# Glu product and the first depth half of MLP units two to four: one 512-column matmul with the weights' high part in place of two of 256

## The chip, the cores and the metric

The kernel runs on one core of one Trainium2 chip. The metric is the device time of one execution in microseconds, the median of several runs. TensorE (PE in the profile) multiplies, VectorE (DVE) and ScalarE (ACT) do the elementwise work, GpSimd (POOL) little, and SyncE (SP) issues most DMAs. PEld is PE's loading of weights, which overlaps its matmuls.

## The reference, cut to what matters

One decoder block on 256 tokens of width 2048, in float32: a state-space branch and an attention branch, gated and merged, then an MLP of width 8192, both behind RMS norms whose scale and shift come from a conditioning vector c.

```
mod = silu(c) @ w_ada + b_ada                 # sh1, sc1, g1, sh2, sc2, g2
h = rms_norm(x) * (1 + sc1) + sh1
u, q, k, v, ga, gb = split(h @ w_in)
y = gelu(ssm(u));  y_ssm = y * sigmoid(y @ w_glu + b_glu)      # w_glu: 1024 x 1024
merged = sigmoid(ga) * (y_ssm @ w_proj_ssm) + sigmoid(gb) * (attention(q, k, v) @ w_proj_attn)
x = x + g1 * (merged @ w_out)
h2 = rms_norm(x) * (1 + sc2) + sh2
x = x + g2 * (square(relu(h2 @ w_ff1)) @ w_ff2)                # w_ff1: 2048 x 8192
out = rms_norm(x)
```

## The kernel before, in words

**Products in two parts.** Every large product is taken in float32 parts that PE multiplies fast: a number is a high part (the rounded cast) plus a low part (what is left). Of the four part products three are summed: high x high, high weight x low activation, low weight x high activation. `split` (L179) makes the parts of a tile of weights: a cast on ACT (L184, whi) and a subtraction on DVE (L186, wlo).

**Weights as a stream.** `stream` (L190) loads a tile of 128 x 1024 float32 (512 KB, seven buffers wraw), splits it (four buffers each of whi and wlo) and yields it. Load and split get a priority of 300 (OFF) ahead of their place in the program. With a list of two depth tiles `load` (L170) takes 128 x 512 of each instead: the same 512 KB, in rows of 2 KB and not 4 KB. A tile scheduler of the language orders each engine's instructions by priority and by a model of their times; `after` pins one instruction behind another.

**Three forms of product.** They differ in which operand is held in the array and how wide the other one is.
- `steps_n` (L303) holds the activations and streams the weights, 512 columns.
- `steps_t` (L255, called by `gemm_t`) holds a 128 x 128 block of weights and streams the 256 tokens. A tile is eight blocks, three matmuls of 256 columns each: L270 whi x high activation, L271 whi x low activation, L272 wlo x high activation. Two blocks share a PSUM bank, so 1024 columns of weights take four banks.
- `gemm_d` (L279) holds a block of weights too, but streams high and low activations beside each other: L289 is one matmul of 512 columns with whi, L293 one of 256 with wlo, which lands on the second half of the bank. A bank then belongs to one block of 128 weight columns, so four banks hold 512 columns of weights, and the result is the sum of the bank's two halves. It takes the weights in pairs of depth tiles. Activations must lie as [depth tile, high/low, token].

**Banks.** `four` (L109) gives four banks. While `turn` is None they come from one rotation of five ("mm"); three others ("ax") are for transposes and the like. From L1683 on, groups alternate between four of the first kind and one of the first with the three others.

**Order of the program around the change.** After the input products and the attention and scan (to about 430 us): `proj_attn(0)` (L1402); the glu product (L1412, `gemm_t`, 8 tiles), whose banks go straight into sigmoids (L1418), a multiply (L1421) and a split into gg; `proj_attn(1)`; the product of gg with w_proj_ssm; w_out; then the MLP. Its first product is cut into eight units of 1024 columns. For the first four units (NP = 4) the first half of the depth is taken early, while the second half of the activations h2h is not there yet (loop at L1653): unit one (g = 0) over 4 depth tiles, before the shift is known, units two to four (g = 1 to 3) over 8 tiles with `gemm_t`. An ACT copy of 128 x 512 per bank (L1663) takes the result into `part`. The rest of the depth and the other units run later in `ff1` (L1545, `gemm_d`): there a unit is two groups of 512 columns, and its banks go out by an ACT copy of one half (L1557) and a DVE add of the other (L1558), or, onto a `part`, by two DVE adds (L1554, L1555).

**The conditioning beside it.** mod is worked out on DVE beside the products: a job of the lane "ada" loads 512 KB of w_ada and, one tile later, multiplies and sums it (L391). `step` (L155) runs after each tile of a stream and adds the lane's rate to its credit; a job starts per whole credit. The rates are constants: R4 for the 8 tiles of the last v product, RS0 for the 16 tiles of the next one, RS3 and RPA around glu, RM for units two to four. 96 jobs must be done before `make_h` (L1679) makes the second half of h2h; `flush` (L1677) issues what is left.

Of the kernel before, what the change touches and what calls it, by code (L numbers as in the profile page):

```python
# [13 lines left out]
F32R = mybir.dt.float32r  # L14
I32 = mybir.dt.int32
AF = mybir.ActivationFunctionType
# [3 lines left out]
P = 128  # L20
S = 256
# [26 lines left out]
R1 = .75  # L48
R2 = .75
R3 = .25  # L50
R4 = .7
R5 = .9
RS0 = .4
RSM = .2
RS2 = .25
RS3 = .7
# [2 lines left out]
RSS = .41  # L59
RPA = .6  # L60
RWO = .76
RM = 1.0
NP = 4
TW = 3
TF = 6
# [12 lines left out]
class Kern:  # L78
# [200 lines left out]
    def gemm_d(self, src, kts, c0, x2):  # L279
        nc = self.nc  # L280
        banks = self.four("pd")
        pairs = self.pairs(list(kts))
        n = len(pairs)
        for i, (ks, hi, lo) in enumerate(self.stream(src, pairs, c0)):
            last = i == n - 1
            cut = lambda blk, k: slice(512 * k + blk * P, 512 * k + (blk + 1) * P)

            def high(blk, k):
                nc.tensor.matmul(banks[blk], hi[:, cut(blk, k)], x2[:, ks[k], :, :], start=i + k == 0, stop=False,  # L289
                                 skip_group_check=True)  # L290

            def low(blk, k):
                self.mm = nc.tensor.matmul(banks[blk][:, S:2 * S], lo[:, cut(blk, k)], x2[:, ks[k], 0, :], start=False,  # L293
                                           stop=last and k == 1, skip_group_check=True)

            for blks in [(b,) for b in range(4)] if last else [range(4)]:
                for f in (high, low):
                    for blk in blks:
                        for k in range(2):
                            f(blk, k)  # L300
        return banks

    def steps_n(self, src, kts, c0, xh, xl, koff=0, tail=1, mid={}, homes=(), seed=None):  # L303
        nc = self.nc
# [705 lines left out]
    def body(self):  # L1010
        nc, a, v = self.nc, self.a, self.nc.vector
# [61 lines left out]
        with self.tc.high_priority(offset=OF1):  # L1073
# [15 lines left out]
            a2 = self.slot("A2", [P, KT, 2, S], F32R, name="ah")  # L1089
# [13 lines left out]
            h = self.big.tile([P, 2, S], F32, name="htmp", tag="htmp", bufs=1)[:, 0]  # L1103
# [140 lines left out]
        def qkvu(u, after=None, spare=False, mid={}):  # L1244
            which, g0, g1 = u
            self.spare = spare
            f = self.gemm_n if which in (2, 4) else self.gemm_t
            banks = f(*place(*u), self.ah, self.al, seed=seeds(which) if g0 else None, mid=mid)
            if after:
                self.prime(*place(*after))  # L1250
            evac(which, banks, g0)
# [88 lines left out]
        qkvu((1, 3, 3), (2, 3, 3))  # L1340
        self.lanes["ada"][1] = R4
        self.lane("tz", [lambda h=h: self.bias_load(h) for h in range(0, H, 2)], .4, .6)
# [28 lines left out]
        self.lane("m", heads[4:-4] + [table0] + heads[-4:] + [start] + bgl, RAT, 1.0)  # L1371
        self.lanes["ada"][1] = RS0

        for i in range(1, 4):
# [3 lines left out]
            banks = self.gemm_n(win, range(KT), c0, self.ah, self.al, tail=2)  # L1378
# [16 lines left out]
        def proj_attn(cg):  # L1395
            banks = self.gemm_n(a["w_proj_attn"][0], range(8), cg * 1024, yh, yl)
            for b in range(4):
                c = cg * 1024 + (b % 2) * 512
                d = gb[:, b // 2, c:c + 512]
                v.tensor_mul(d, d, banks[b])  # L1400

        proj_attn(0)  # L1402
        self.lanes["ada"][1] = RPA
        yy = self.slot("VT", [P, 2, 8, S], F32R, name="yy")
        yT = self.yT.rearrange("p s k c -> p k s c")
        sc4 = lambda z: z.rearrange("p k (c s) -> p k s c", s=4)
        self.gate, self.hgate = self.done[-4]
        for k in range(4):
            self.split(sc4(yy[:, 0, 2 * k:2 * k + 2]), sc4(yy[:, 1, 2 * k:2 * k + 2]), yT[:, 2 * k:2 * k + 2])
        self.gate = self.hgate = None  # L1410
        self.gates = [(None, None), self.done[-1]]
        banks = self.gemm_t(a["w_glu"][0], range(8), 0, yy[:, 0], yy[:, 1])  # L1412
        gg = self.slot("QT", [P, 2, 8, S], F32R, name="gg")
        sg = self.slot("S5", [P, 4, 2, S], name="sg")
        for b in range(4):
            t = sg[:, b]
            for k in range(2):
                nc.scalar.activation(t[:, k], banks[b][:, k * S:(k + 1) * S], AF.Sigmoid,  # L1418
                                     bias=self.bglu[:, 2 * b + k:2 * b + k + 1])
            s = slice(2 * b, 2 * b + 2)  # L1420
            v.tensor_mul(sc4(t), sc4(t), yT[:, s])  # L1421
            self.split(gg[:, 0, s], gg[:, 1, s], t)
        proj_attn(1)
        m2 = self.slot("A2", [P, 2, KT, S], F32R, name="mh")
        mh, ml = m2[:, 0], m2[:, 1]
# [11 lines left out]
        for cg in range(2):  # L1437
            banks = self.gemm_n(a["w_proj_ssm"][0], range(8), cg * 1024, gg[:, 0], gg[:, 1])
            if cg:
                self.flush("turn")  # L1440
            for b in (0, 2, 1, 3):
                c = cg * 1024 + (b % 2) * 512
                d, e = ga[:, b // 2, c:c + 512], gb[:, b // 2, c:c + 512]
# [9 lines left out]
        for cg in range(2):  # L1453
# [6 lines left out]
            banks = self.gemm_n(a["w_out"][0], range(KT), cg * 1024, mh, ml, tail=TW if cg else 1)  # L1460
# [3 lines left out]
            with self.hot():  # L1464
                for b in range(4):
                    t, c = b // 2, slice(cg * 1024 + (b % 2) * 512, cg * 1024 + (b % 2) * 512 + 512)
# [16 lines left out]
        with self.hot():  # L1483
# [3 lines left out]
            a2 = self.slot("A2", [P, KT, 2, S], F32R, name="h2h")  # L1487
# [39 lines left out]
        w1, w2 = a["w_ff1"][0], a["w_ff2"][0]  # L1527
        ffs = {}

        def square(g, f, t, b):  # L1530
            last = self.done[-1][1]
            for k in range(2):
                q = t[:, b, k * S:(k + 1) * S]
                if g:
                    q = t[:, b] if k == 0 else None
                if q is not None:
                    with self.after(last):
                        nc.scalar.activation(q, q, AF.Relu, bias=0.0 if g else wb[:, 2 * b + k:2 * b + k + 1])
            nc.scalar.activation(t[:, b], t[:, b], AF.Square)
            self.split(f[:, 0, 2 * b:2 * b + 2].rearrange("p k s -> p (k s)"),  # L1540
                       f[:, 1, 2 * b:2 * b + 2].rearrange("p k s -> p (k s)"), t[:, b])
# [3 lines left out]
        def ff1(g, k0=0, part=None):  # L1545
            f = self.slot(("VT", "QT")[(1 - g if g < 2 else g) % 2], [P, 2, 8, S], F32R, name="ff")
            ffs[g] = f
            t = part if part is not None else self.slot(("T", "SV")[g % 2], [P, 4, 512], name="fr")
            for h in range(2):
                banks = self.gemm_d(w1, range(k0, KT), g * 1024 + 512 * h, a2)  # L1550
                for b in range(4):
                    q = t[:, 2 * h + b // 2, (b % 2) * S:(b % 2 + 1) * S]
                    if part is not None:
                        v.tensor_add(q, q, banks[b][:, 0:S])  # L1554
                        v.tensor_add(q, q, banks[b][:, S:2 * S])  # L1555
                    else:
                        nc.scalar.copy(q, banks[b][:, S:2 * S])  # L1557
                        v.tensor_add(q, q, banks[b][:, 0:S])  # L1558
                self.flush("act")
                self.lane("act", [nop, nop] + [lambda b=b: square(g, f, t, b) for b in (2 * h, 2 * h + 1)], 1.0)  # L1560

# [91 lines left out]
        for g in range(NP):  # L1653
            part = self.slot(("S4", "T", "SV", "S5")[g], [P, 4, 512], name="part")
            if g:
                banks = self.gemm_t(w1, range(0, 8), g * 1024, self.ah, self.al)
            else:
                wh, wl = [self.slot(n, [P, 4, 1024], F32R, name="wf") for n in ("VT", "QT")]
                banks = self.gemm_t(w1, range(0, 4), 0, hp[:, 0], hp[:, 1], mid={2: h_first, 3: h_second},
                                    homes=[(wh[:, k, :], wl[:, k, :]) for k in range(4)])  # L1660
            for b in range(4):
                if g:
                    nc.scalar.copy(part[:, b, :], banks[b])  # L1663
                else:
                    with self.after(hs["h0"]):
                        v.tensor_mul(part[:, b, :].rearrange("p (k s) -> p k s", s=S),
                                     banks[b].rearrange("p (k s) -> p k s", s=S),
                                     self.R[:, None, :].to_broadcast([P, 2, S]))
            parts.append(part)
            if g == 0:  # L1670
                self.lanes["ada"][1] = RM
                self.agate = None
            if g == 1:
                scale2(2, 0, self.done[-1][0])
                scale2(3, 0, self.done[-1][0])
                self.ada_bcast(B2[:, 0:4], b2r, self.mm)
# [64 lines left out]
```

## Time and profile before

| | before |
|---|---|
| median of 3 runs | 1356.16 us (1355.76 to 1356.31) |
| the profiled execution | 1356.04 us, of which the span from first to last instruction is 1354.3 us |
| PE, DVE, ACT busy | 1342.8, 1038.2, 751.1 us |
| glu product | from 451.5 to 474.6 us |
| units two to four, first depth half | from 647.0 to 718.7 us |
| DMA | 357 MB, 264 GB/s over the span |

Times in rows are microseconds from the span's start. In a group's row, what follows the bar is its busy time, the mean duration of one in nanoseconds, then the idle time of the engine just before and what ended it. In a timeline row, the first two numbers are start and duration, "x8" counts instructions merged into the row, and square brackets hold the idle time ahead and its releaser. Matmuls are pipelined: their durations overlap, so the time of one is read from start to start. A row of a window gives the busy time of each engine with its number of instructions, then PE's granted clock, the DMA engines' mean share and the rate in GB/s.

### The profile page before, as it was taken

The page shows a single profiled execution, that of the slowest core. Times are in us where ns is not written, and L with a number is a line of the kernel's source. Part 1 is how long each engine was busy: PE and PEld are TensorE (multiplying, and loading weights), DVE is VectorE, ACT ScalarE, POOL GpSimd, SP SyncE. Part 2 cuts the span into 40 slices and gives each one's busy share as a digit, 9 for nine tenths or more (in the row PEclk, how much of TensorE's full clock was granted, in tenths as well). Part 3 has the DMA queues.
Part 4 walks back from the last instruction along what each step waited for, and adds up shares of the span by engine and source line. Part 5 has one row for each costly group of instructions (what it writes and reads, how often), then busy time and mean ns, then how long its engine had stood idle before and what let it go on. Part 6 is the DMA issues. An engine that isn't in the chain of part 4 may idle for free.

```text
span 1354.3 us, 21608 instructions
## 1 busy us (share of the span) xinstructions
PE 1342.8 (99%) x8276; PEld 1167.6 (86%) x8276; DVE 1038.2 (77%) x1441; ACT 751.1 (55%) x1045; POOL 49.0 (4%) x105
## 2 busy tenths in 40 slices
PE   9999999999999999999999999999999999999997
PEld 8898899788888988888998888888888888888886
DVE  7888998677987888988888967686765555565687
ACT  7768656766558543455546656353554544535544
POOL 0000004200004000000000000000000000000000
PEclk9999999999999999999999999999999999999999
DMA  9999977975568888997899897888878666566552
GB/s 377 407 408 409 389 252 210 306 241 180 159 215 262 314 283 300 334 337 290 291 342 339 296 235 263 220 281 258 276 243 230 190 187 197 187 188 198 176 196 83
DMA packets 116856, 357.09 MB, mean 264 GB/s; under 512 B 16728, under 2 KB 16864, under 8 KB 116464
## 3 DMA queue, kind: packets, MB, share of 16 engines
q1 hardware_dynamic: 113056, 348.83, 76.5%
q0 software_dynamic: 3120, 5.70, 1.4%
q8 instruction: 65, 1.06, 0.3%
q10 hardware_dynamic: 576, 1.18, 0.3%
q14 instruction: 39, 0.32, 0.1%
HBM read 350.79 MB, written 2.51 MB: 261 GB/s over the span
## 4 chain that ended last, share of the span: by engine, by line
PE 95%; ACT 2%; DMA 2%; DVE 1%; issue 0%; SPq 0%; ACTq 0%; DVEq 0%
PE pn L327 18%; PE pn L329 18%; PE pn L331 18%; PE pd L289 14%; PE pd L293 7%; PE pt L270 6%; PE pt L272 6%; PE pt L271 6%; DMA wraw<-in_w_in_dram 1%; PE ys L992 1%; ACT whi L184 1%; DMA xt<-in_xt_dram 0%; PE trh L834 0%; PE vr L954 0%; PE rk L794 0%
## 5 line engine op out<-in xcount | busy, mean ns | idle before, releaser
L186 DVE TENSOR_TENSOR wlo<-wraw,whi 128x1024 fp32r<-128x1024 f32 x448 | 546.2, 1224 | 254.4 <-ACT whi L184 253.0
L184 ACT CAST whi<-wraw 128x1024 fp32r<-128x1024 f32 (+1 forms) x449 | 467.3, 1051 | 479.6 <-PE pn L329 214.3
L289 PE MATMUL pd<-h2h,whi 128*128 128x512 f32 x800 | 207.3, 393 | 0.2 <-ACT whi L184 0.2
L327 PE MATMUL pn<-whi,ff 128*128 128x512 f32 x496 | 193.3, 390 | 0.0
L329 PE MATMUL pn<-whi,ff 128*128 128x512 f32 x496 | 193.3, 390 | 0.0
L331 PE MATMUL pn<-wlo,ff 128*128 128x512 f32 x496 | 190.9, 390 | 0.0
L289 PEld LDWEIGHTS pd<-h2h,whi 128*128 128x128 f32 x800 | 141.3, 189 | 22.9 <-ACT whi L184 0.4
L391 DVE SCALAR_TENSOR_TENSOR wraw<-wraw,cb 128x1024 f32<-128x1024 f32 x128 | 156.2, 1221 | 0.0
L327 PE MATMUL pn<-whi,ah 128*128 128x512 f32 x320 | 126.7, 400 | 0.8 <-ACT qk L1216 0.4
L329 PE MATMUL pn<-whi,ah 128*128 128x512 f32 x320 | 125.5, 392 | 0.0
L293 PEld LDWEIGHTS pd<-h2h,wlo 128*128 128x128 f32 x800 | 114.8, 190 | 11.5
L293 PE MATMUL pd<-h2h,wlo 128*128 128x256 f32 x800 | 117.9, 282 | 0.0
L331 PE MATMUL pn<-wlo,ah 128*128 128x512 f32 x320 | 115.9, 392 | 0.4 <-DVE wlo L186 0.4
L331 PEld LDWEIGHTS pn<-wlo,ff 128*128 128x128 f32 x496 | 93.1, 188 | 19.5
L329 PEld LDWEIGHTS pn<-whi,ff 128*128 128x128 f32 x496 | 93.2, 188 | 19.0
L327 PEld LDWEIGHTS pn<-whi,ff 128*128 128x128 f32 x496 | 93.1, 188 | 19.1
L270 PE MATMUL pt<-ah,whi 128*128 128x256 f32 x384 | 105.9, 286 | 0.2 <-DVE tz L611 0.2
L271 PE MATMUL pt<-ah,whi 128*128 128x256 f32 x384 | 104.9, 283 | 0.0
L272 PE MATMUL pt<-ah,wlo 128*128 128x256 f32 x384 | 95.9, 284 | 0.8 <-DVE wlo L186 0.7
L270 PEld LDWEIGHTS pt<-ah,whi 128*128 128x128 f32 x384 | 73.4, 192 | 1.8 <-ACT whi L184 0.7
L271 PEld LDWEIGHTS pt<-ah,whi 128*128 128x128 f32 x384 | 73.4, 192 | 0.2
L327 PEld LDWEIGHTS pn<-whi,ah 128*128 128x128 f32 x320 | 59.9, 188 | 15.3 <-ACT whi L184 1.3
(386 smaller groups left out, 2009.3 us busy)
## 6 DMA issues: line engine op xcount, KB each, us to landing
wraw<-in_w_ff_dram SPq DMA_DIRECT2D x256, 512.0 KB, 4.8
wraw<-in_w_in_dram SPq DMA_DIRECT2D x128, 512.0 KB, 6.1
wraw<-in_wat_dram SPq DMA_DIRECT2D x128, 512.0 KB, 5.9
ahm<-in_wat_dram SPq DMA_DIRECT2D x48, 512.0 KB, 10.2
wraw<-in_w_out_dram SPq DMA_DIRECT2D x32, 512.0 KB, 6.5
wraw<-in_w_proj_attn_dram SPq DMA_DIRECT2D x16, 512.0 KB, 5.7
wraw<-in_w_proj_ssm_dram SPq DMA_DIRECT2D x16, 512.0 KB, 6.4
ahm<-in_wan_dram SPq DMA_DIRECT2D x8, 512.0 KB, 10.6
```

Source lines behind the costliest of these rows:

```text
L184: h = self.nc.scalar.copy(hi[:, c], src[:, c])
L186: s = self.nc.vector.tensor_sub(lo, src, hi.bitcast(F32))
L270: nc.tensor.matmul(o, hi[:, c], xh[:, kx, :], start=st, stop=False, skip_group_check=True)
L271: nc.tensor.matmul(o, hi[:, c], xl[:, kx, :], start=False, stop=False, skip_group_check=True)
L272: self.mm = nc.tensor.matmul(o, lo[:, c], xh[:, kx, :], start=False, stop=sp, skip_group_check=True)
L289: nc.tensor.matmul(banks[blk], hi[:, cut(blk, k)], x2[:, ks[k], :, :], start=i + k == 0, stop=False, skip_group_check=True)
L293: self.mm = nc.tensor.matmul(banks[blk][:, S:2 * S], lo[:, cut(blk, k)], x2[:, ks[k], 0, :], start=False, stop=last and k == 1, skip_group ...
L327: nc.tensor.matmul(o, xh[:, kx, tk], hi[:, c], start=q == 0 and not full, stop=False, skip_group_check=full)
L329: nc.tensor.matmul(o, xl[:, kx, tk], hi[:, c], start=False, stop=False, skip_group_check=full)
L331: self.mm = last = nc.tensor.matmul(o, xh[:, kx, tk], lo[:, c], start=False, stop=q == n - 1, skip_group_check=full)
L391: v.scalar_tensor_tensor(w, w, 1.0, self.cb[:, (i % 2) * 1024:(i % 2 + 1) * 1024], op0=OP.mult, op1=OP.mult, accum_out=pc[:, i:i + 1])
L992: nc.tensor.matmul(p[q, c], self.cc[q, i, j].rearrange("p s c -> p (s c)"), self.sri[q, b % 2, i, c], start=i == 0, stop=False)
```

## The change

The glu product and units two to four of the first depth half go from `gemm_t` to `gemm_d`, each unit as two groups of 512 columns. A new function `join` takes the banks out: ACT copies the second half, DVE adds the first. It also stands in for the same two lines in `ff1`. The layout of yy turns to [depth tile, high/low, token]. In glu the sigmoids now read the joined sums, in two halves of the columns. Unit one stays as it is. Three rates of the lane "ada" change: R4 from 0.7 to 0.8, RS0 from 0.4 to 0.55, RM from 1.0 to 0.8.

```diff
-R4 = .7
+R4 = .8
-RS0 = .4
+RS0 = .55
-RM = 1.0
+RM = .8
...
+    def join(self, banks, dests):
+        for o, d in zip(banks, dests):
+            self.nc.scalar.copy(d, o[:, S:2 * S])
+            self.nc.vector.tensor_add(d, d, o[:, 0:S])
...
-        yy = self.slot("VT", [P, 2, 8, S], F32R, name="yy")
+        yy = self.slot("VT", [P, 8, 2, S], F32R, name="yy")
...
-            self.split(sc4(yy[:, 0, 2 * k:2 * k + 2]), sc4(yy[:, 1, 2 * k:2 * k + 2]), yT[:, 2 * k:2 * k + 2])
+            self.split(sc4(yy[:, 2 * k:2 * k + 2, 0]), sc4(yy[:, 2 * k:2 * k + 2, 1]), yT[:, 2 * k:2 * k + 2])
...
-        banks = self.gemm_t(a["w_glu"][0], range(8), 0, yy[:, 0], yy[:, 1])
...
-        for b in range(4):
-            t = sg[:, b]
-            for k in range(2):
-                nc.scalar.activation(t[:, k], banks[b][:, k * S:(k + 1) * S], AF.Sigmoid,
-                                     bias=self.bglu[:, 2 * b + k:2 * b + k + 1])
-            s = slice(2 * b, 2 * b + 2)
-            v.tensor_mul(sc4(t), sc4(t), yT[:, s])
-            self.split(gg[:, 0, s], gg[:, 1, s], t)
+        for h in range(2):
+            banks = self.gemm_d(a["w_glu"][0], range(8), 512 * h, yy)
+            self.join(banks, [sg[:, 2 * h + b // 2, b % 2] for b in range(4)])
+            for b in (2 * h, 2 * h + 1):
+                t = sg[:, b]
+                for k in range(2):
+                    nc.scalar.activation(t[:, k], t[:, k], AF.Sigmoid, bias=self.bglu[:, 2 * b + k:2 * b + k + 1])
+                s = slice(2 * b, 2 * b + 2)
+                v.tensor_mul(sc4(t), sc4(t), yT[:, s])
+                self.split(gg[:, 0, s], gg[:, 1, s], t)
...
             if g:
-                banks = self.gemm_t(w1, range(0, 8), g * 1024, self.ah, self.al)
+                for h in range(2):
+                    self.join(self.gemm_d(w1, range(0, 8), g * 1024 + 512 * h, a2),
+                              [part[:, 2 * h + b // 2, (b % 2) * S:(b % 2 + 1) * S] for b in range(4)])
...
-            for b in range(4):
-                if g:
-                    nc.scalar.copy(part[:, b, :], banks[b])
-                else:
+                for b in range(4):
```

More of the change, by code (lines that the diff above doesn't have):

```diff
@@ L1556, in ff1 @@
                     else:
-                        nc.scalar.copy(q, banks[b][:, S:2 * S])
-                        v.tensor_add(q, q, banks[b][:, 0:S])
+                        self.join([banks[b]], [q])
                 self.flush("act")
```

## The prediction

> **What bounds the kernel now.** I read the page first: busy times, slices, chain.
>
> ```profile
> PE 1342.8 (99%) x8276; PEld 1167.6 (86%) x8276; DVE 1038.2 (77%) x1441; ACT 751.1 (55%) x1045; POOL 49.0 (4%) x105
> ...
> PE 95%; ACT 2%; DMA 2%; DVE 1%; issue 0%; SPq 0%; ACTq 0%; DVEq 0%
> ```
>
> PE is busy for 99% of the span, 95% of the chain that ended last is PE, and every window below has its clock at 1.00. A busy PE may still be a waiting one, so the next view is PE's waits from 200 to 760 us, where every changed line lies.
>
> ```profile
> PE pn L331 <- DVE wlo L186: 0.4, 1, 0.4
> PE pn L327 <- ACT whi L184: 0.3, 1, 0.3
> PE pd L289 <- ACT whi L184: 0.2, 1, 0.2
> ```
>
> Three waits, 0.9 us in 560. So the time here is the time between matmul starts. A change gains by making PE's stream shorter, and loses wherever PE has to wait anew. The first is a count; the second needs the neighbours' load by stage:
>
> ```profile
> core 0: us, PE busy (x) PEld busy (x) DVE busy (x) ACT busy (x) POOL busy (x), PEclk, DMA share, GB/s
> 451.50:474.60 23.10, 23.10 (x194) 23.07 (x193) 19.75 (x28) 10.20 (x14) 0.00 (x0) 1.00 0.92 313
> 474.60:496.30 21.70, 21.70 (x97) 17.97 (x97) 20.35 (x27) 11.32 (x16) 0.00 (x0) 1.00 0.80 275
> 647.00:670.50 23.50, 23.50 (x200) 23.50 (x198) 21.56 (x32) 11.71 (x17) 0.00 (x0) 1.00 0.74 268
> 670.50:694.60 24.10, 24.10 (x205) 24.10 (x202) 18.55 (x26) 10.69 (x14) 0.00 (x0) 1.00 0.99 366
> 694.60:718.70 24.10, 23.92 (x201) 23.72 (x199) 20.23 (x31) 11.59 (x17) 0.00 (x0) 1.00 0.96 341
> 949.95:994.60 44.65, 44.65 (x257) 39.28 (x256) 30.30 (x38) 22.67 (x30) 0.00 (x0) 1.00 0.82 272
> ```
>
> The first row is the glu product, rows four to six are units two to four, and the last is a unit that already runs in the new form. In the rows that change, VectorE is at 77 to 92% and the DMA engines at up to 99%: PE is the bound, with two others close behind.
>
> **The stream.** A tile of 128 x 1024 weights (or a pair, twice 128 x 512) is 8 blocks of 128 x 128. Now a block takes three matmuls of 256 columns (L270 to L272); in the new form one of 512 and one of 256 (L289, L293). Both have 768 columns.
>
> ```profile
> 451.52 0.28 PE L270 MATMUL pt<-yy,whi 128*128 128x256 f32 x1
> ...
> 474.56 0.40 PE L327 MATMUL pn<-whi,yh 128*128 128x512 f32 x1
> 949.95 0.62 PE L289 MATMUL pd<-h2h,whi 128*128 128x512 f32 x2
> 994.60 0.40 PE L327 MATMUL pn<-whi,ff 128*128 128x512 f32 x1
> 721.61 2.00 PE L289 MATMUL pd<-h2h,whi 128*128 128x512 f32 x8
> 723.45 1.11 PE L293 MATMUL pd<-h2h,wlo 128*128 128x256 f32 x8
> 724.40 0.46 PE L289 MATMUL pd<-h2h,whi 128*128 128x512 f32 x1
> ```
>
> The durations in these rows overlap their neighbours; what counts is the step from start to start. The glu product's 8 tiles run from 451.52 to 474.56: 23.04 / 8 = 2.880 us a tile. The clean unit in the new form runs its 16 pairs from 949.95 to 994.60: 2.791 us a pair. The three rows at 721 us show why: 8 matmuls of 512 columns step (723.45 - 721.61) / 8 = 230 ns, 8 of 256 columns 119 ns; the old form's 24 of 256 columns step 2.880 / 24 = 120 ns. Two old ones are 240 ns, one wide one is 230: a matmul has some 10 ns of fixed cost, and a third of the matmuls go. The change covers 8 tiles of glu and 3 x 8 of the units: 32 x (2.880 - 2.791) = 2.86 us. With nothing hiding it, that is the gain: 0.21%. No idle time of PE is removed beyond it, except perhaps the 0.2 us at L289 in the list of waits.
>
> The Trainium skill ("TensorE: Matmul & The Clock Gate", Back-to-back issue gap) gives N / 2.4 + about 2.5 ns between isolated warm matmuls. By that, an estimate, a block would save 2.6 ns and the change 0.7 us. This trace has 10 ns of fixed cost in its place, and the sum goes by the trace.
>
> **Banks.** In these stages one group of products takes four of five rotating banks, and a unit now has two groups (512 weight columns each) where it had one. So block 1, 2, 3 of a new group wait for bank 0, 1, 2 of the last one, and they come up 0.46, 0.92 and 1.38 us into it (two 230 ns steps each). A bank is now freed by an ACT copy, then a DVE add. That pair exists already in the later units:
>
> ```profile
> 451.41 0.72 DVE L1400 TENSOR_TENSOR gb<-gb,pn 128x512 f32<-128x512 f32 x1
> 452.01 1.25 DVE L186 TENSOR_TENSOR wlo<-wraw,whi 128x1024 fp32r<-128x1024 f32 x1
> 453.14 1.91 DVE L1400 TENSOR_TENSOR gb<-gb,pn 128x512 f32<-128x512 f32 x3
> ...
> 1169.11 0.37 ACT L1557 COPY fr<-pd 128x256 f32<-128x256 f32 x1 [0.60 <-PE pd L293]
> 1169.69 0.95 DVE L1558 TENSOR_TENSOR fr<-fr,pd 128x256 f32<-128x256 f32 x2
> 1170.91 0.42 DVE L1558 TENSOR_TENSOR fr<-fr,pd 128x256 f32<-128x256 f32 x1 [0.28 <-ACT fr L1557]
> 1171.00 0.40 PE L327 MATMUL pn<-whi,ff 128*128 128x512 f32 x1
> ```
>
> In the last four rows banks 0 to 2 are free at 1170.1, 1170.6 and 1171.3, the next group starts at 1171.00. Under the new order they would be wanted at 1171.46, 1171.92 and 1172.38: 1.1 to 1.4 us to spare, with DVE at 68% (30.30 of 44.65). One split ahead of the add (1.25 us, the row at 452.01) eats that slack and costs 0.1 us or so; two cost 2.5 - 1.1 = 1.4 us. DVE's load rises here: 24 adds x 0.42 = 10.1 us come to units two to four, some 3 of the reductions of 1.2 us go (below), so 60.3 + 6.2 = 66.5 us in 69.6, 96%. In glu and the product after it 8 adds bring 40.1 to 43.4 us in 44.1.
>
> A late bank need not be paid for, though. In the first three rows the second bank of the product before glu came free 0.7 us after 453.14, some 0.9 us after glu's fifth block would have wanted it (451.52 + 4 x 0.36), and the glu product still has its 120 ns a step on the average: the order of instructions had other blocks at that place. Each new wait also holds what stands behind it. A copy waits in ACT's queue for its bank's last matmul, and the next casts stand behind the copy:
>
> ```profile
> 717.12 0.59 ACT L1663 COPY part<-pt 128x512 f32<-128x512 f32 x1 [5.01 <-PE pt L272]
> 718.71 2.11 PE L289 MATMUL pd<-h2h,whi 128*128 128x512 f32 x8 [0.18 <-ACT whi L184]
> ```
>
> At the end of unit four the first tile's cast ran behind such a copy, and PE waited 0.18 us for it. The old ends of units two and three show no such wait; with the new form there are six ends for three, and one in glu: 0 to 7 x 0.2 = 1.4 us. An add waits in DVE's queue for its copy, with splits behind it that have four buffers of lead.
>
> Over nine entries into a group of the new form I take 0.3 us for both together, bounds 0 and 9 x 1.4 = 12.6, to which the casts could add their 1.4.
>
> **Pacing.** R4 and RS0 move 0.1 x 8 + 0.15 x 16 = 3.2 load-and-reduce jobs of the ada lane into the stretch from 238 to 304 us; RM takes 0.2 x 24 = 4.8 from units two to four. All 24 that run there now end just in time:
>
> ```profile
> L391 DVE SCALAR_TENSOR_TENSOR wraw<-wraw,cb 128x1024 f32<-128x1024 f32 x24 | 29.1, 1220 | 0.0
> 715.58 1.22 DVE L391 SCALAR_TENSOR_TENSOR wraw<-wraw,cb 128x1024 f32<-128x1024 f32 x1
> 720.02 0.16 DVE L1052 TENSOR_TENSOR B<-pcs,pack 128x4 f32<-128x4 f32 x1
> 723.62 0.69 DVE L186 TENSOR_TENSOR h2h<-htmp,h2h 128x512 fp32r<-128x512 f32 x1 [0.16 <-ACT h2h L184]
> ```
>
> The last reduction (715.58) makes the shift column at 720.02, which makes the activations of depth tiles 12 and 13 at 724.31 (723.62 + 0.69), and PE takes them at 724.40, its third pair after 718.71. There is no slack in that chain. Afterwards 20.8 jobs are left for 19.2 paces, so one or two instead of one fall to the flush at L1677; unit four ends some 2.1 us earlier (24 x 0.089), and four adds stand in DVE's queue at its end. Against that fewer loads go before. The traffic is 8 tiles and 6.4 to 7 jobs of 0.524 MB in 22.3 us, 338 to 352 GB/s; the window at 670.50, all in rows of 4 KB, at share 0.99 moved 366, the one of the new form, whose pairs come in rows of 2 KB, 272 at 0.82, or 332 at full share. So the loads are still at the limit. Cost: from -0.2 (the wait at 718.71 goes) to 2.4 us (two reductions late); I take 0.6.
>
> The 3.2 jobs come in where the DMA engines stand at 1.03, and right behind it PE is idle for 0.7 us, the 0.3 and 0.4 of its list of waits:
>
> ```profile
> 250.00:260.00 10.00, 10.00 (x48) 8.25 (x48) 7.29 (x12) 4.26 (x6) 0.00 (x0) 1.00 1.03 361
> 260.00:270.00 10.00, 9.28 (x42) 6.89 (x41) 8.02 (x18) 9.92 (x26) 0.00 (x0) 1.00 0.86 314
> ```
>
> One more load of 0.524 MB at 361 GB/s is 1.45 us on the queue that the casts stand behind. Bounds -0.7 (both waits go) to +1.4; I take 0.2. The rest of the moved jobs falls after 270 us, where the DMA engines have room.
>
> **What is hidden.** The glu result is needed late:
>
> ```profile
> L186 DVE TENSOR_TENSOR gg<-sg,gg x4: 700/702/702, 480.3 to 482.1; 128x512 fp32r<-128x512 f32 x4
> L327 PE MATMUL pn<-whi,gg x64: 387/390/477, 496.3 to 540.6; 128*128 128x512 f32 x64
> ```
>
> It is ready at 482.8 and wanted at 496.3: 13.5 us cover the 8 copies (0.37) and 8 adds, 6.3 us if they ran in a row, and less as half of them move into the product itself. If that cover went, proj_ssm would start late by the difference. ACT, at half load, takes 24 copies of half the width for 12. The strided activations yy change order, not size: nothing.
>
> **Sum.** -2.86 + 0.3 + 0.6 + 0.2 = -1.76 us on the profiled execution's 1356.04, so 1354.28; the median of the runs is 0.12 above it, so 1354.4.
>
> **Rivals.** (1) Nothing new waits: 1356.16 - 2.86 = 1353.3, or 1353.1 if the 0.2 us at 718.71 goes too. For it: PE hid every late bank and late low part so far. Against: three resources at 92 to 99% at once. 0.27. (2) The banks, on the other side: at the entries of units two to four and glu two DVE instructions stand ahead of the adds, 1.4 us each. From 0.6 us an entry (5.6 us in nine) the change is slower by over 0.2%; at the full price it is 1356.16 - 2.86 + 12.6 = 1365.9. For it: DVE at 96 to 98% and five banks instead of the eight that the later units alternate over. Against: the late bank at 453 that cost nothing. 0.15. The Trainium skill ("Perfetto Trace Analysis", Matmul Optimizations) asks that all 8 PSUM banks be used; by that this rival gains, but the trace has old groups on five banks without a stall. (3) The wide matmul steps at 240 ns in these stages, not 230, so the fixed cost saved is nil: 1356.16 + 1.1 = 1357.3. All rows of the new form speak against it; 0.06. By the Trainium skill's "TensorE: Matmul & The Clock Gate" (Back-to-back issue gap), with its 2.5 ns, it would be near here, at 1356.6, an estimate. (4) My forecast, parts of the gain given back: 0.52.
>
> **The numbers.** 0.2% is 2.7 us, about what a measurement of this kernel can tell from no change. Rival 1 lies just beyond it and takes nearly all of "faster": 0.28; rival 2 is "slower": 0.15; the rest, 0.57, is within. The forecast's own range is 1353.5 (below it is rival 1) to 1357.4 (the pacing's upper bounds, 2.4 and 1.4). The range for 8 in 10 goes down to 1352.8 (rival 1 with the attention waits partly gone) and up into the cheap end of rival 2, 0.55 us an entry with the pacing's 0.6 and 0.2: 1359.0.
>
> **What would show it.** Right: pt<-yy and pt<-h2h,whi gone; glu's stage near 22.3 us for 23.0 and units two to four near 69.6 for 71.7, with PE's waits list as short as now; the adds of the new joins ending less than 1.4 us after the bank's last matmul. Wrong: idle time before L289 ended by a DVE add, or by the activations h2h after unit four, or a longer wait at 266 us; or steps of 240 ns at L289.

## The result and the profile after

The changed kernel takes 1363.7 us, the median of 6 runs (1362.3 to 1365.7), against 1355.96 us for the kernel before beside it: a ratio of 1.0057 [1.0044, 1.007], so 7.7 us slower where 1.8 us faster was forecast. Its profiled execution has a span of 1361.2 us, 6.9 longer than before. From L302 on, its lines stand five further down (L391 is L396, L834 is L839); the copy and the add of `join` are L305 and L306.

The page of the changed kernel, busy times and chain:

```profile
PE 1342.6 (99%) x8020; PEld 1152.0 (85%) x8020; DVE 1047.1 (77%) x1473; ACT 756.1 (56%) x1065; POOL 49.1 (4%) x105
...
PE 89%; DVE 4%; DMA 4%; ACT 2%; issue 1%; SPq 0%; ACTq 0%; DVEq 0%
```

256 matmuls fewer (8276 before), and PE busy for the same time: the 2.86 us that the stream saved came back as longer steps. On top of that PE's idle time, span less busy, went from 11.5 to 18.6 us. The 99% of both pages shows neither. The chain does: PE's share went from 95 to 89%, DVE's and the DMAs' from 1 and 2 to 4% each. The list of PE's waits from 200 to 760 us shows where (us in all, times, longest):

```profile
PE pd L293 <- DVE wlo L186: 2.3, 3, 0.9
PE pd L289 <- DVE part L306: 2.2, 4, 0.6
PE sco L865 <- ACT bp L769: 1.1, 1, 1.1
PE pd L289 <- ACT whi L184: 0.8, 1, 0.8
PE pn L332 <- ACT v L1221: 0.7, 1, 0.7
PE pn L332 <- DVE sg L306: 0.6, 1, 0.6
```

Before, it held 0.9 us in all. Now four of six lines are of the changed stages: PE waits for the adds that free banks (part and sg, L306) and for the parts of its weights. By stages, from the first matmul of each to the first of the next:

| stage | before | after | difference | forecast |
|---|---|---|---|---|
| scores to the product before glu | 182.19 | 183.03 | +0.84 | +0.2 |
| glu | 23.04 | 23.72 | +0.68 | -0.7 + banks |
| the product after glu | 21.78 | 23.10 | +1.32 | 0 |
| unit two to the second MLP product | 127.68 | 131.62 | +3.94 | -2.1 + 0.6 + banks |

The remaining stages add 0.2 together. Matmuls do step as forecast, 230 ns the wide ones and 119 the narrow ones, where nothing waits. From 640 to 735 us, the steps above those nominal times sum to 7.3 us, before to 1.3.

The timeline of the changed kernel at the entry into unit three's second group (start, duration, engine, line, operation):

```profile
686.47 1.01 ACT L305 COPY part<-pd 128x256 f32<-128x256 f32 x3
...
686.91 0.62 PE L289 MATMUL pd<-h2h,whi 128*128 128x512 f32 x2
687.37 0.40 PE L293 MATMUL pd<-h2h,wlo 128*128 128x256 f32 x2
687.60 0.63 PE L289 MATMUL pd<-h2h,whi 128*128 128x512 f32 x2
...
688.12 1.22 DVE L396 SCALAR_TENSOR_TENSOR wraw<-wraw,cb 128x1024 f32<-128x1024 f32 x1
...
688.30 0.63 PE L289 MATMUL pd<-h2h,whi 128*128 128x512 f32 x2
...
689.27 1.22 DVE L186 TENSOR_TENSOR wlo<-wraw,whi 128x1024 fp32r<-128x1024 f32 x1
...
690.40 1.22 DVE L396 SCALAR_TENSOR_TENSOR wraw<-wraw,cb 128x1024 f32<-128x1024 f32 x1
...
690.54 0.50 PE L293 MATMUL pd<-h2h,wlo 128*128 128x256 f32 x2 [0.91 <-DVE wlo L186]
...
691.55 1.41 DVE L306 TENSOR_TENSOR part<-part,pd 128x256 f32<-128x256 f32 x4
...
692.11 0.70 PE L289 MATMUL pd<-h2h,whi 128*128 128x512 f32 x2 [0.60 <-DVE part L306]
```

Three things are to be read from it. ACT has copied the banks out from 686.47 on, but the adds run only at 691.55: reductions and splits stand ahead of them in DVE's queue. The new group starts at 687.60 (the pair at 686.91 is the last block of the group ahead). Until 692.11 PE works on the one free bank alone: two wide and two narrow matmuls, then the next pair of tiles, 0.70 us a pair (687.60 to 688.30 and on) where four open banks take 2.79. So the low parts of four pairs are wanted within 3 us, and PE waits 0.91 us for one. Then it waits 0.60 for the next bank, and the DVE work that delayed the adds stood ahead of that low part as well. Glu's second group shows the same (0.91 us for wlo at 466.57).

### The profile page after: what moved, and what is told of

It reads as the page before. It is cut to its first block, busy times and chain, and to the rows that moved or that the text cites. A ratio compares the mean times of both kernels' runs of the same rounds, so it can differ in the third digit from the quotient of the medians.

```text
span 1361.2 us, 21163 instructions
## 1 busy us (share of the span) xinstructions
PE 1342.6 (99%) x8020; PEld 1152.0 (85%) x8020; DVE 1047.1 (77%) x1473; ACT 756.1 (56%) x1065; POOL 49.1 (4%) x105
## 4 chain that ended last, share of the span: by engine, by line
PE 89%; DVE 4%; DMA 4%; ACT 2%; issue 1%; SPq 0%; ACTq 0%; DVEq 0%
PE pn L332 18%; PE pn L334 17%; PE pn L336 17%; PE pd L289 16%; PE pd L293 8%; PE pt L272 3%; PE pt L270 3%; PE pt L271 3%; DMA wraw<-in_w_in_dram 2%; DVE wlo L186 1%; DVE wraw L396 1%; DMA wraw<-in_w_ff_dram 1%; PE ys L997 1%; ACT whi L184 1%; DMA rt<-cmp 0%
## 5 line engine op out<-in xcount | busy, mean ns | idle before, releaser
L289 PE MATMUL pd<-h2h,whi 128*128 128x512 f32 x992 | 267.4, 394 | 3.0 <-DVE part L306 2.2
L289 PEld LDWEIGHTS pd<-h2h,whi 128*128 128x128 f32 x992 | 170.9, 189 | 27.8 <-PE pd L289 1.8
L293 PEld LDWEIGHTS pd<-h2h,wlo 128*128 128x128 f32 x992 | 149.1, 190 | 21.2 <-DVE wlo L186 2.5
L293 PE MATMUL pd<-h2h,wlo 128*128 128x256 f32 x992 | 154.7, 282 | 1.4 <-DVE wlo L186 1.4
L396 DVE SCALAR_TENSOR_TENSOR wraw<-wraw,cb 128x1024 f32<-128x1024 f32 x128 | 156.0, 1220 | 0.0
```

The costliest lines, as they stand in the source:

```text
L396: v.scalar_tensor_tensor(w, w, 1.0, self.cb[:, (i % 2) * 1024:(i % 2 + 1) * 1024], op0=OP.mult, op1=OP.mult, accum_out=pc[:, i:i + 1])
```

## The experiments

**Theory.** The banks (rival 2): with five of them, groups that come twice as often, and a DVE add as the last hop of each bank, PE waits at the entries. Rivals: the new rates of the ada lane cost the time; the new form itself does; or one of glu and units alone.

### Eight banks

The changed kernel, with groups that alternate over all eight banks in glu and units two to four:

```diff
+        self.turn = False
         for h in range(2):
             banks = self.gemm_d(a["w_glu"][0], range(8), 512 * h, yy)
...
+        self.turn = None
         proj_attn(1)
...
             if g:
+                self.turn = False
```

> The changed kernel, but its new groups alternate over all eight PSUM banks (four of the rotation, then one of it and the three others), in glu and in units two to four. Theory banks (the add that frees a bank stands in VectorE's queue behind reductions and splits, and five banks give no second set): the waits of L289 for L306 go, 2.2 us as listed and about as much again in restarts, so 1357 to 1360 us, with units two to four near 70 to 71 us. Theory VectorE load (wlo late whatever the banks): 1362 to 1364, the waits of L293 for wlo stay or grow. Theory pacing: no change, 1363.

1360.8 us (1360.2 to 1361.8), ratio 1.0036 [1.0023, 1.0049]. The product after glu is back at its old 21.78 us, glu is 0.2 longer than before and not 0.7, and the waits for banks and parts in the units are gone. Yet the units' stage still loses 3.68 us, all of it behind unit four. The timeline there:

```profile
715.51 1.09 PE L839 MATMUL trh<-ident,xs 128*128 128x128 f32 x8 [0.35 <-DVE part L306]
717.28 1.09 PE L839 MATMUL trh<-ident,xs 128*128 128x128 f32 x8 [0.68 <-ACT htmp L849]
721.30 3.62 PE L289 MATMUL pd<-h2h,whi 128*128 128x512 f32 x8 [2.93 <-DVE h2h L186]
724.72 1.21 PE L293 MATMUL pd<-h2h,wlo 128*128 128x256 f32 x8
725.76 0.63 PE L289 MATMUL pd<-h2h,whi 128*128 128x512 f32 x2
```

PE is idle three times, 3.96 us in all: twice around the transposes, which now share their banks with the units' groups (the first wait is for part, L306), then 2.93 us for the activations h2h made from them. And then eight wide matmuls take (724.72 - 721.30) / 8 = 427 ns each. The windows tell why (busy times, then granted clock, DMA share and rate):

```profile
715.00:721.30 6.30, 2.34 (x18) 1.71 (x17) 5.39 (x11) 3.56 (x6) 0.00 (x0) 1.00 0.99 349
721.55:724.85 3.30, 3.30 (x9) 2.53 (x9) 0.69 (x1) 2.45 (x5) 0.00 (x0) 0.50 0.85 307
```

After 6.3 us in which PE was busy for 2.3, the clock is at 0.50 for 3.3 us. A second mechanism, then. Idle time ended by h2h is among the prediction's signs of being wrong, but it has no late transposes and no change of the clock.

### The old rates

The changed kernel with R4, RS0 and RM as before.

```diff
-R4 = .8
+R4 = .7
...
-RS0 = .55
+RS0 = .4
...
-RM = .8
+RM = 1.0
```

> The changed kernel with the three old rates (R4 0.7, RS0 0.4, RM 1.0). Theory pacing: most of the loss goes, 1355 to 1357 us. Theory banks: the 0.8 us before glu comes back, but VectorE carries 3 more reductions in units two to four, so 1362 to 1365. Theory VectorE load: 1364 to 1367, slower than with the new rates.

1368.7 us (1365.1 to 1369.0), 1.0087 [1.0069, 1.0105]: taking the new rates back makes the loss larger, 0.87% for 0.57% (the intervals just touch). The units' stage loses 8.3 us for 3.94; PE waits there 3.2 us for wlo, 2.4 for whi and 1.3 for part. With the old RM more loads of the ada lane go between those of the weights, which fits the later parts.

### The rates alone

The kernel before with the three new rates, and nothing else.

> The kernel before with the three new rates and nothing else. Theory pacing: a large part of the loss is here, 1360 us or more. Theories banks and VectorE load: only the attention stretch moves, by the 0.8 us that the trace of the changed kernel shows ahead of the products after it, so 1356 to 1357.

1363.0 us (1362.3 to 1365.0), 1.0049 [1.0033, 1.0066]. By themselves the rates cost nearly as much as the whole change. Of it, 6.69 us lie behind unit four, in the picture of the eight banks: idle for 0.77 and 3.36 us until h2h is there, then a long stretch at half clock:

```profile
723.20:729.90 6.70, 5.52 (x17) 4.75 (x18) 1.81 (x4) 4.22 (x7) 0.00 (x0) 0.50 0.48 157
```

The scale and shift columns are not late, B is ready at 714.81 (before: 720.02). Late are the transposes (trh) that `make_h` does ahead of them. Their first and last start, in the kernel before, the changed one, the eight banks and the rates alone:

```profile
L834 PE MATMUL trh<-ident,xs x32: 270/273/274, 641.7 to 707.7; 128*128 128x128 f32 x32
```

```profile
L839 PE MATMUL trh<-ident,xs x32: 270/272/277, 644.4 to 678.9; 128*128 128x128 f32 x32
```

```profile
L839 PE MATMUL trh<-ident,xs x32: 271/272/330, 641.9 to 718.1; 128*128 128x128 f32 x32
```

```profile
L834 PE MATMUL trh<-ident,xs x32: 271/273/328, 642.9 to 720.7; 128*128 128x128 f32 x32
```

Before, half of those for depth tiles 8 to 15 ran at 694 us, the rest by 708; here all of them run behind unit four. The program has them behind units two to four, and the tile scheduler moved them ahead before and in the changed kernel, and not in these two.

Another 1.26 us are lost in glu, which has the old form here:

```profile
453.37 1.23 DVE L391 SCALAR_TENSOR_TENSOR wraw<-wraw,cb 128x1024 f32<-128x1024 f32 x1
...
454.51 1.89 DVE L1400 TENSOR_TENSOR gb<-gb,pn 128x512 f32<-128x512 f32 x3
...
455.26 0.38 PE L270 MATMUL pt<-yy,whi 128*128 128x256 f32 x1 [0.77 <-DVE gb L1400]
```

The multiplies that free the banks of the product before glu ran at 453.14 in the kernel before; here a reduction stands ahead of them, and PE waits for the bank.

### Glu alone

The kernel before with the new form in glu only, old rates.

```diff
-                for h in range(2):
-                    self.join(self.gemm_d(w1, range(0, 8), g * 1024 + 512 * h, a2),
...
+                banks = self.gemm_t(w1, range(0, 8), g * 1024, self.ah, self.al)
+                for b in range(4):
+                    nc.scalar.copy(part[:, b, :], banks[b])
```

> The kernel before with the new form in glu alone, units and rates as before. Theory banks: glu and the product after it lose what the changed kernel's trace shows there, 0.7 + 1.3 us, so 1357.5 to 1358.5. Theory VectorE load: the same size. If the loss lies in the units alone: 1355.3, glu's share of the stream gained.

1357.8 us (1356.6 to 1359.7), 1.0012 [1.0002, 1.0021]. Glu's stage is shorter by 0.69 us, the forecast's 0.71. The product after it is longer by 1.23 us, most of it one wait for a low part at its start:

```profile
476.52 0.50 PE L336 MATMUL pn<-wlo,yh 128*128 128x512 f32 x1 [0.94 <-DVE wlo L186]
```

### Eight banks and early transposes

As the first experiment, and the transposes for depth tiles 8 to 11 are put behind unit three.

```diff
+            if g == 2:
+                self.make_h(xs, range(8, 12), A2, B2)
         self.flush()
...
-        for c in (2, 3):
-            self.make_h(xs, range(4 * c, 4 * c + 4), A2, B2)
+        self.make_h(xs, range(12, 16), A2, B2)
```

> The changed kernel with all eight banks in glu and units two to four (as in e1), and the transposes that make depth tiles 8 to 11 of h2h issued right after unit three instead of after unit four. Theory A (what is left of e1's loss, 3.7 us from unit two to the last product's first pair, is late transposes: with fewer loads the last 32 transposes stand in one block behind unit four, so the activations come 3 us late and the clock falls to 0.50 behind that idle time): the stage from unit two to the last product falls by 3 to 5 us, its idle time before L289 ended by h2h is under 0.5 us, no row of 427 ns steps follows, and the time is 1355 to 1357, with attention's 0.7 us still lost. Rival B (the activations are late because the last reduction of the scale and shift columns is late, whatever the place of the transposes): the idle time of about 3 us and the 427 ns steps stay, 1360 to 1361.

1354.9 us (1353.5 to 1357.5, 10 runs), 0.9991 [0.9982, 1.0]: the loss is gone, and the units' stage is 1.84 us shorter than before, of 2.14 forecast for the stream. PE's waits from 200 to 760 us, and the timeline where the changed kernel enters unit two's second group:

```profile
PE pn L332 <- ACT v L1221: 0.7, 1, 0.7
PE sco L865 <- ACT bp L769: 0.5, 1, 0.5
PE pd L289 <- DVE gb L1405: 0.5, 1, 0.5
PE pd L289 <- DVE part L1563: 0.4, 1, 0.4
```

```profile
661.34 2.00 PE L289 MATMUL pd<-h2h,whi 128*128 128x512 f32 x8
663.18 1.11 PE L293 MATMUL pd<-h2h,wlo 128*128 128x256 f32 x8
664.14 2.00 PE L289 MATMUL pd<-h2h,whi 128*128 128x512 f32 x8
```

All four banks take part in every pair: x8 and x8, where the changed kernel has x2 and x2. No half clock is left.

### The rates with early transposes

The kernel before, with the new rates and the same edit of `make_h`.

> The kernel before with the three new rates, as e3 (1363.0), and with the transposes for depth tiles 8 to 11 issued right after unit three. Glu and the units keep the old form. Theory A (e3's 6.7 us behind unit four come from the transposes' place): half of the transposes run before unit four's end, idle time before the first pairs of the last product falls from 4.1 us to under 1.5, and no 427 ns steps follow or fewer; 1356.5 to 1359.5. Rival B (the reductions are late): unchanged at 1362 to 1364.

1356.7 us (1355.6 to 1357.9), 1.0007 [0.9997, 1.0016], from 1363.0 without the edit. The list of PE's waits from 640 to 760 us is empty. So the place of the transposes is what the rates alone lost by behind unit four; glu's stage still loses 0.69 us.

### Adds ahead of the reductions

The changed kernel; in units two to four a reduction that falls due within a group is held until the group's copies and adds are issued.

```diff
+        if not self.hold:
+            self.settle(self.tno)
...
-                    self.join(self.gemm_d(w1, range(0, 8), g * 1024 + 512 * h, a2),
+                    self.join(self.gemm_d(w1, range(0, 8), g * 1024 + 512 * h, a2, True),
```

> The changed kernel on five banks; in units two to four the load-and-reduce jobs that fall due inside a group are held until that group's copies and adds have been issued, so that the adds stand ahead of the reductions in VectorE's queue. Theory A1 (the adds that free banks wait behind reductions): PE's waits for part L306 (2.2 us in the changed kernel) fall under 0.8, the unit stage gains 1.5 to 4 us, 1359 to 1362. Rival A2 (the adds wait behind the splits wlo, or VectorE is simply full in the model that orders the queue): the waits move to wlo but the sum of extra step time from 640 to 735 us stays near 7.3, and the time stays at 1362.5 to 1365.

1363.4 us (1361.9 to 1364.1), 1.0058 [1.0042, 1.0075]. The units' stage loses 1.93 us and not 3.94, and the waits there are shorter (L308 is the add here), but the total stands where it was:

```profile
PE pd L291 <- DVE part L308: 1.0, 1, 1.0
PE pd L291 <- ACT whi L185: 1.0, 1, 1.0
PE pd L295 <- DVE wlo L187: 0.6, 2, 0.4
```

The profiled execution lost 1.4 us in the product of gg with w_proj_ssm, which this edit doesn't touch. The median of the runs shows no gain; on the order in DVE's queue alone this stays inconclusive.

### Short reductions

The changed kernel, with 24 reductions near the units taken over 128 of 1024 terms, so those conditioning sums lack seven eighths. Banks, order of the program and loads stay.

```diff
+                m = 128 if vec in (3, 4) and k0 + (vec == 3) > 8 and k0 != 4 else 1024
+                v.scalar_tensor_tensor(w[:, 0:m], w[:, 0:m], 1.0, self.cb[:, (i % 2) * 1024:(i % 2) * 1024 + m],
```

> The changed kernel on five banks, with the 24 reductions that run from unit one's end to unit four taken over 128 of their 1024 terms (this leaves out seven eighths of those conditioning sums), so about 1.0 us x 21 of VectorE's load goes from units two to four and nothing else. Theory A1/A2 together (VectorE's queue is what makes the banks and the low parts late): waits for part and wlo nearly vanish, extra step time 640 to 735 us falls from 7.3 to under 3; what is then left is e1's late transposes at the end, so 1358 to 1361. Rival C (the five banks are short by themselves: the copy and the add take longer than the 0.46 us that a block leaves, whatever else is queued): waits for part L306 and for ACT stay, 1362 to 1365.

1356.9 us (1355.8 to 1359.0), 1.0009 [0.9999, 1.0018]. The list of waits from 640 to 760 us is empty, and the units' stage is 2.48 us shorter than before. The window from 640 to 735 us, in the changed kernel and in this one:

```profile
640.00:735.00 95.00, 90.62 (x543) 78.50 (x543) 82.21 (x136) 51.65 (x82) 0.00 (x0) 1.00 0.82 285
```

```profile
640.00:735.00 95.00, 95.00 (x579) 84.31 (x578) 69.08 (x147) 53.94 (x85) 0.00 (x0) 1.00 0.88 309
```

With DVE at 69 us of 95 instead of 82, five banks are enough. What is left of the loss lies around glu, where no reduction was cut: its stage and the two after it lose 0.71, 1.32 and 0.93 us. Before, DVE was at 80.8 us in the same window and PE didn't wait, as ACT alone freed the banks.

### The units alone

The kernel before with the new form in units two to four only, old rates.

> The kernel before with the new form in units two to four alone (five banks, glu in the old form, the three old rates). Theory: what the units lose is their own, from late adds and late low parts on five banks; the stage from unit two to the last product's first pair is longer than before's by 5 to 9 us with waits for part, wlo and whi as in e2, glu and proj_attn(1) are as before: 1361 to 1365. Rival: the units' loss comes from the glu's new form or from the rates, so the units alone bring their stream gain of 2.1 us: 1353.5 to 1355.

1365.4 us (1363.0 to 1366.6), 1.0068 [1.0053, 1.0083]. Glu is as before, the units' stage loses 10.5 us. Waits from 640 to 760 us, then two windows:

```profile
PE pd L293 <- DVE wlo L186: 3.2, 4, 1.1
PE pd L289 <- ACT whi L184: 2.2, 2, 1.3
PE pd L289 <- DVE part L306: 1.6, 3, 0.6
PE pd L289 <- DVE h2h L186: 0.6, 1, 0.6
```

```profile
659.20:662.60 3.40, 1.80 (x8) 0.91 (x6) 2.40 (x4) 2.14 (x5) 0.00 (x0) 1.00 1.02 386
662.60:669.30 6.70, 5.59 (x16) 4.72 (x17) 5.58 (x13) 1.05 (x1) 0.00 (x0) 0.50 1.03 382
```

The waits for parts are larger than those for banks, and here they bring the clock down as well, for 6.7 us; the same waits in the old-rates kernel (2.9 us idle between 660 and 665) did not.

### Eight banks, old rates, without and with early transposes

> The new form in glu and units two to four on eight banks, with the three old rates: the form by itself, without bank waits and without the moved load-and-reduce jobs. Theory: no wait for part or wlo in 640 to 710 us. The stream gain (2.86 us) arrives, but the jobs are as late as my pacing step said, since all of them stay in stages that are shorter: the rest is idle time of PE at the end of unit four of 0 to 3 us; attention is as before: 1353.5 to 1357. Rival (the late transposes appear whenever the banks no longer stall, whatever the rates): 2.9 us idle before L289 and a stretch of 427 ns steps as in e1, 1357 to 1361.

1359.9 us (1358.9 to 1361.7), 1.0032 [1.002, 1.0044]. Glu's stage is 0.72 us shorter and the product after it unchanged: glu's whole stream gain, with no wait, where the same eight banks at the new rates lost 0.2 us. In the units no wait for banks or parts is left except at the end, where the late transposes stand:

```profile
PE pd L289 <- DVE h2h L186: 2.1, 1, 2.1
PE trh L839 <- ACT htmp L849: 1.3, 1, 1.3
PE trh L839 <- DVE part L306: 0.6, 1, 0.6
```

Half clock follows from 718.75 to 725.45 (0.50 in that window), and the stage loses 4.71. So the late transposes come without the new rates too, as the rival on record has it. It is no rule, though: the kernel before, glu alone and the short reductions have no stalls for banks in the units either, and their transposes are done by 709 us.

> As e5 (eight banks, transposes for depth tiles 8 to 11 right after unit three), with the three old rates. Theory: the new rates cost attention and glu entry 0.3 to 1.2 us and bring at most 1 us at unit four's end once the transposes are early. So 1353.5 to 1355.5, within 1 us of e5 (1354.9). Rival (the lower rate is needed at unit four's end once the units are shorter): idle time of 1 to 3 us before L289 ended by h2h, 1356 to 1359.

1355.4 us (1354.7 to 1359.7), 1.0004 [0.9994, 1.0013]. Early transposes take 4.6 us off again. One wait of 1.5 us for whi stays behind unit four (716.31), where the old RM loads until the end; it is absent with the new rates.

### Jobs moved elsewhere

As eight banks with early transposes, but R4 and RS0 old, and RSM and RS2 raised, so that the moved jobs fall between 304 and 430 us.

```diff
-RSM = .2
-RS2 = .25
+RSM = .35
+RS2 = .4
```

> As e5, but the jobs taken from units two to four go to the stretch from 304 to 430 us, where the DMA engines stand at 0.55 to 0.68 (RSM .35 for .2, RS2 .4 for .25), in place of the attention stretch (R4 and RS0 old). Theory: no new wait at 262 and 267 us, units as in e5 or 0.3 better: 1353.3 to 1354.5, below e5 by 0.3 to 1.2. Rival (the added loads meet the casts there too): a new wait between 304 and 430 us, 1355 to 1357.

1355.7 us (1353.5 to 1359.8, 10 runs), 0.9999 [0.9989, 1.0009]. The units' stage reaches -2.55 us and no wait is left from 640 to 760, yet the median doesn't fall: the profiled execution is the fastest of ten that spread over 6 us. No version here is faster than before by 0.2%; the best is 0.09%, at the edge of what the runs tell.

## Why the prediction was wrong

**The stream: right.** Wide matmuls step at 230 ns in all of these kernels where nothing waits. At the old rates glu gave 0.69 us of 0.71 by itself on five banks and 0.72 on eight, and the units, at the new RM and with the banks out of the way, 1.84 and 2.55 of 2.14. The side estimate of 2.6 ns a block and 0.7 us comes to 2.5 and 0.6 when it is worked out again; the sum doesn't use it.

**The banks: the step that failed.** "Over nine entries into a group of the new form I take 0.3 us for both together". Measured as stage against stream, the product after glu lost 1.32 us and units two to four 3.94 + 2.14, 7.4 us together (the pacing took none of it at unit four's end: the list has no wait for h2h there). Glu itself fell short by 0.68 + 0.71; how much of that is the banks' can't be told, because five banks at the old rates left it 0.69 (glu alone) or 0.29 us (the old rates) of its gain, and the rates alone cost it 1.26. With or without it, that is 0.8 to 1.0 us an entry, inside the bounds of 0 to 12.6 and past the 0.6 from which rival 2 decided. Rival 2 had the main part of the mechanism; at 687 to 691 us four DVE instructions, not two, stood ahead of the adds. That DVE's reductions and the five banks are both needed in the units is shown: eight banks or short reductions each take the units' waits for banks and parts away. From 640 to 735 us DVE is at 85.2 us of 95 with eight banks and early transposes, at 69.1 with short reductions.

Two things in the working were off. The late bank at 453 us, "that cost nothing", came some 0.9 us late; the one at 692.11 came 4.5 us after its group had started on another. On one bank a group uses up its weights at four times the pace (0.70 us a pair for 2.79), and their low parts come from the same DVE; the waits for parts (2.3 us for wlo) are as large as those for adds (2.2). The old form has that pace too (two blocks, six matmuls at 120 ns, 0.72 us a tile for 2.88), but in the units ACT alone freed its banks. And one more reduction ahead of the late bank at 453 us made PE wait 0.77 us in the rates alone. The other thing is the slack of the banks: it was read at 1169 us, where DVE stands at 52% (5.75 of 11.00 us from 1160 to 1171; the 68% beside it is of the unit at 949), and carried into stages where it stands at 83 to 90%.

The Trainium skill ("Perfetto Trace Analysis", Matmul Optimizations) asks that all 8 PSUM banks be used. The prediction set it aside by the old form's five banks without a stall; with the DVE add in the path and DVE this busy the runs agree with the rule. At the old rates the units' stage loses 8.31 us on five banks and gains 0.55 on eight with early transposes; with short reductions five banks were enough.

**Pacing at unit four's end: nil, by luck.** The forecast of 0.6 us, within -0.2 to 2.4, looked at the last reduction. In the changed kernel PE did not wait behind that chain; on five banks at the old rates it did, 0.6 us for h2h at 729 and 731 us (the old rates, the units alone). What the forecast left out are the transposes ahead of it, whose place the scheduler chooses, and they cost 6.7 us in the rates alone. In the changed kernel they ran at 675 to 679 us, earlier than before. So the losses of the rates and of the form don't add: 6.6 us for the rates alone, 9.4 for the units alone, 7.7 for the change. Why the scheduler moves them ahead in some kernels is not in the traces and stays open; none of the three kernels in which they were late had stalls for banks before unit four's end, but three in which they were early had none either.

**Pacing in the attention stretch: unclear.** 0.84 us instead of 0.2, with waits of 1.1 and 0.7 us at 262 and 268. With the same rates the stage differs from before by -0.3 to +0.9 us over the other runs, and with the old ones by -0.7 to +0.5, one profiled execution each. The size can't be told.

**Pacing around glu: put at nothing.** The prediction let the rest of the moved jobs fall "after 270 us, where the DMA engines have room" and looked no further. The rates alone cost glu's stage 1.26 us, and 0.69 with early transposes, by a reduction ahead of the multiplies that free its banks. That, and not the form, is why eight banks give nothing in glu at the new rates (+0.21 and +0.03 us, with waits of 0.7 and 0.5 us for gb) and 0.72 us at the old.

**Cover behind glu: right.** gg was not waited for at its start; the loss in the product after glu came from banks and low parts.

## What to carry to other kernels

When a product's result gets one more hop on its way out of PSUM, price the hop by the queue of the engine that does it, at the load of that very stage, and count the entries: twice as many groups on the same banks are twice as many chances to wait. A bank that is late and free of cost shows that the order has other work at that place; ask how long that work lasts and what it will demand sooner. And where a scheduler places the work, a change of rates or stalls can move instructions that the edit doesn't name: look at where the transposes, not only the last reduction, stand.

## What the runs showed of the hardware

PE's granted clock fell to 0.50 after stretches in which PE was idle for about half of the time or more, and stayed there for some 3.3 us (eight banks, wide matmuls at 427 ns) or 6.7 us (three other runs). The Trainium skill ("TensorE: Matmul & The Clock Gate", Part 1: The HAM clock gate) has half rate after an idle window of about 3.4 us, free-running; the lengths of 3.3 and 2 x 3.35 us fit one and two such windows. But the window need not be all idle: in the units alone PE was busy for 1.80 of the 3.40 us ahead of the fall, and its longest unbroken idle time until then was 0.87 us. Where the limit lies stays open, for the old-rates kernel kept its clock at the same place with PE busy for less of the time:

```profile
660.00:665.00 5.00, 2.06 (x10) 1.13 (x9) 3.30 (x8) 3.18 (x6) 0.00 (x0) 1.00 1.02 349
```

At half clock 5.59 us of matmuls do the work of 2.8, an estimate from the two clocks, so in the units alone stalls of about a microsecond close together cost 2.8 us more than they last.
